# A streaming prefix log-sum-exp on one core: unrolled schedule against a hardware loop of four turns

## The chip, the core and the metric

The kernel runs on one core of a Trainium2 chip. The core has a matrix engine (PE), a vector engine (DVE), an activation engine (ACT), a general engine (POOL) and a sync engine (SP), which here does nothing but issue DMA transfers. Sixteen DMA engines move data between the device memory (DRAM) and the on-chip memory. The metric is the device time of one execution in microseconds.

## The reference

Input `x` and output have the shape [4, 4096, 4128] in fp32: four batches, 4096 time steps, 4128 independent columns. Along the time steps each column keeps a running log-sum-exp:

```python
out[:, 0, :] = x[:, 0, :]
for t in range(1, S):
    mx = np.maximum(out[:, t - 1, :], x[:, t, :])
    out[:, t, :] = mx + np.log(np.exp(out[:, t - 1, :] - mx) + np.exp(x[:, t, :] - mx))
```

That is the logarithm of the running sum of exp(x). Both kernels compute it in that form: Exp, prefix sum along the steps, Ln.

## The kernel before

A batch's 4096 steps are cut into tiles. A tile has r consecutive steps per partition, on 128 partitions, so 128 x r steps by all 4128 columns; r is `R` = 3 (6.34 MB) except for one tile of r = 2 per batch, since 4096 / 128 = 32 = 10 x 3 + 2. The tile of r = 2 is the first of batch 0 and the last of the other three (L150 to L153). That makes 11 tiles per batch, 44 in all. Each tile is loaded into one of four buffers, worked on in place, and stored from there.

The columns of a tile are cut into four chunks of 1024 (`CH`); the 32 columns left over, the tail, belong to the last chunk. The work on a chunk:

- `act` with Exp on ACT (L106), over all r steps; for the last chunk it covers the tail too;
- `own` on DVE (L77): r-1 adds that form the running sum inside each partition's r steps;
- `head` on PE (L74): two matrix products of 512 columns with the constant matrix `excl`, which sum each partition's last step over all partitions above it, into the chunk's own PSUM tile `above`;
- `add_above` on DVE (L77, one add of r x 1024 columns): adds that sum to every step;
- `pick` on PE (L74): two products with the constant `pick`, which copy partition 127's last step, now the running total, into `above` for the next tile, where `head` accumulates onto it;
- `act` with Ln on ACT, and after the last chunk's Ln the store.

The tail has no PSUM of its own: `above_t` is a piece of the last chunk's `above`. So its total is kept in SBUF in `carry_t` (L146), and for the last chunk `tail_head`, `tail_add` and half of `pick` stand in an order of their own: the tail's sum is written only after `add_above` has read that PSUM, and the last chunk's `pick` has to wait for `tail_add`.

The order of the work is written out by hand and fully unrolled (L183 to L199): for chunk g it issues `own` and `head` of chunk g+1, Exp of chunk g+2, `finish` (tail) and Ln of chunk g-1, and then `add_above` and `pick` of chunk g. This runs on without a break over tiles and batches: Exp of the next tile's first three chunks stands on ACT before the last chunk's Ln of this tile. A framework sets the semaphores.

SP's queue holds the three loads at the start, and then for each tile its store, followed by the load of the tile three further on (L173 to L177). That load goes to the buffer of the tile before the one just stored, so it waits until that store has landed. The constants `excl` and `pick` are made on POOL (L16 to L31), `carry_t` is cleared on DVE (L69).

Of the kernel before, what the change touches and what calls it, by code (L numbers as in the profile page):

```python
# [1 line left out]

# [4 lines left out]

FP32 = mybir.dt.float32
ACT = mybir.ActivationFunctionType
P = 128  # L10
R = 3
CH = 1024
MM = 512


def _constants(nc, pool):  # L16

    excl = pool.tile([P, P], FP32, name="excl")
    nc.gpsimd.memset(excl, 1.0)  # L19

    nc.gpsimd.affine_select(  # L21
        out=excl, in_=excl, pattern=[[1, P]], compare_op=mybir.AluOpType.is_ge,
        fill=0.0, base=-1, channel_multiplier=-1,
    )
    pick = pool.tile([P, P], FP32, name="pick")
    nc.gpsimd.memset(pick, 0.0)  # L26
    nc.gpsimd.affine_select(  # L27
        out=pick, in_=pick, pattern=[[0, P]], compare_op=mybir.AluOpType.not_equal,
        fill=1.0, base=-(P - 1), channel_multiplier=1,
    )  # L30
    return excl, pick  # L31


@with_exitstack
def kernel(
    ctx: ExitStack,
    tc: tile.TileContext,
    x: bass.AP,
    out: bass.AP,
):  # L40

    nc = tc.nc
    B, S, D = x.shape
    assert S % P == 0  # L50
    n_main = D // CH
    tail = D - n_main * CH
    t0 = n_main * CH
    last = n_main - 1

    nc.scalar.preload_act_table_set("natural_log_exp_and_others")  # L56
    consts = ctx.enter_context(tc.tile_pool(name="consts", bufs=1))
    excl, pick = _constants(nc, consts)

    bufs = 4  # L60
    xpool = ctx.enter_context(tc.tile_pool(name="xpool", bufs=bufs))
    cpool = ctx.enter_context(tc.tile_pool(name="cpool", bufs=1))
    psum = ctx.enter_context(tc.tile_pool(name="psum", bufs=1, space=bass.MemoryType.PSUM))

    above = [psum.tile([P, CH], FP32, name=f"above{c}") for c in range(n_main)]

    above_t = above[last][:, CH - MM:CH - MM + tail]
    carry_t = cpool.tile([P, tail], FP32, name="carry_t")
    nc.vector.memset(carry_t, 0.0)  # L69

    ctx.enter_context(tc.manual_schedule())

    def mm(pt, w, rhs, start=False, stop=False):
        nc.tensor.matmul(pt, lhsT=w, rhs=rhs, start=start, stop=stop, skip_group_check=True)  # L74

    def add(o, a, b):
        nc.vector.tensor_tensor(out=o, in0=a, in1=b, op=mybir.AluOpType.add)  # L77

    class Step:


        def __init__(self, b, row, r):
            self.b, self.row, self.r = b, row, r
            self.first = row == 0
            self.final = row + P * r == S

        def dram(self, t):
            rows = t[self.b, self.row:self.row + P * self.r, :]
            return rows.rearrange("(p j) d -> p j d", j=self.r)

        def load(self):
            full = xpool.tile([P, R, D], FP32, name="xt")
            self.xt = full[:, :self.r, :]
            nc.sync.dma_start(out=self.xt, in_=self.dram(x))  # L94

        def store(self):
            nc.sync.dma_start(out=self.dram(out), in_=self.xt)  # L97

    class Chunk:
        def __init__(self, step, c):  # L100
            self.t, self.c = step, c
            self.a, self.b = c * CH, D if c == last else (c + 1) * CH

        def act(self, func):
            v = self.t.xt[:, :, self.a:self.b]
            nc.scalar.activation(v, v, func)  # L106

        def own(self):

            x = self.t.xt  # L110
            for j in range(1, self.t.r):
                v = x[:, j, self.a:self.b]
                add(v, x[:, j - 1, self.a:self.b], v)

        def head(self):

            t, a = self.t, self.a
            for s in range(0, CH, MM):
                mm(above[self.c][:, s:s + MM], excl, t.xt[:, t.r - 1, a + s:a + s + MM],
                   start=t.first, stop=True)  # L120

        def add_above(self):
            t, a = self.t, self.a
            v = t.xt[:, :, a:a + CH]
            add(v, v, above[self.c].unsqueeze(1).to_broadcast([P, t.r, CH]))

        def pick(self, s0=0, s1=CH):

            t, a = self.t, self.a
            if not t.final:  # L130
                for s in range(s0, s1, MM):
                    mm(above[self.c][:, s:s + MM], pick, t.xt[:, t.r - 1, a + s:a + s + MM],
                       start=True)

        def tail_head(self):
            t = self.t
            if not t.first:
                mm(above_t, pick, carry_t, start=True)
            mm(above_t, excl, t.xt[:, t.r - 1, t0:D], start=t.first, stop=True)

        def tail_add(self):
            t = self.t
            v = t.xt[:, :, t0:D]
            add(v, v, above_t.unsqueeze(1).to_broadcast([P, t.r, tail]))
            if not t.final:
                nc.vector.tensor_copy(carry_t[96:, :], t.xt[96:, t.r - 1, t0:D])  # L146

    steps = []
    for b in range(B):
        n = S // P  # L150
        parts = [R] * (n // R) + ([n % R] if n % R else [])
        if b == 0:
            parts.reverse()  # L153
        row = 0
        for r in parts:
            steps.append(Step(b, row, r))
            row += P * r
        assert row == S

    chunks = [Chunk(s, c) for s in steps for c in range(n_main)]  # L160
    ahead = bufs - 1
    for s in steps[:ahead]:
        s.load()
    stored = 0
    def finish(k):
        if k.c == last:
            k.tail_add()
            k.pick(CH - MM)

    def result(k):  # L170
        nonlocal stored
        k.act(ACT.Ln)
        if k.c == last:  # L173
            k.t.store()
            if stored + ahead < len(steps):
                steps[stored + ahead].load()
            stored += 1  # L177

    chunks[0].act(ACT.Exp)
    chunks[1].act(ACT.Exp)  # L180
    chunks[0].own()
    chunks[0].head()
    for g, k in enumerate(chunks):  # L183
        if g + 1 < len(chunks):
            chunks[g + 1].own()
            chunks[g + 1].head()
        if g + 2 < len(chunks):
            chunks[g + 2].act(ACT.Exp)
        if g:
            finish(chunks[g - 1])  # L190
            result(chunks[g - 1])
        k.add_above()
        if k.c == last:
            k.tail_head()
            k.pick(0, CH - MM)
        else:
            k.pick()
    finish(chunks[-1])
    result(chunks[-1])  # L199


# [1 line left out]
_INS = ['x']  # L203
_OUTS = [((4, 4096, 4128), 'float32')]


# [23 lines left out]
```

The softmax here doesn't subtract the row's maximum and nothing guards it: scores larger than these inputs give would overflow.

## Time and profile before

| what | value |
|---|---|
| median of 10 runs | 1265.37 us (1263.63 to 1266.3) |
| profiled execution | 1265.5 us, its span 1263.8 us |
| moved by DMA | 541.35 MB, 428 GB/s over the span |
| DVE / ACT / PE busy | 980.2 / 923.9 / 755.9 us |
| load, store of r = 3: issue to landing | 41.2 us, 27.0 us (median) |
| load, store of r = 2: issue to landing | 36.2 us, 20.3 us (median) |

The span is the part that the profiler records; 1.7 us of the execution's time lie outside it. Busy time is that of an engine's own instructions. A tile of 6192 KB is listed as issued in one DMA, and the time to landing contains the wait behind earlier transfers in the same queue. GB/s counts reads and writes together.

### The profile page before, as it was taken

The page shows a single profiled execution, that of the slowest core. Times are in us where ns is not written, and L with a number is a line of the kernel's source. Part 1 is how long each engine was busy: PE and PEld are TensorE (multiplying, and loading weights), DVE is VectorE, ACT ScalarE, POOL GpSimd, SP SyncE. Part 2 cuts the span into 40 slices and gives each one's busy share as a digit, 9 for nine tenths or more (in the row PEclk, how much of TensorE's full clock was granted, in tenths as well). Part 3 has the DMA queues.
Part 4 walks back from the last instruction along what each step waited for, and adds up shares of the span by engine and source line. Part 5 has one row for each costly group of instructions (what it writes and reads, how often), then busy time and mean ns, then how long its engine had stood idle before and what let it go on. Part 6 is the DMA issues. An engine that isn't in the chain of part 4 may idle for free.

```text
span 1263.8 us, 4623 instructions
## 1 busy us (share of the span) xinstructions
PE 755.9 (60%) x1512; PEld 287.2 (23%) x1512; DVE 980.2 (78%) x597; ACT 923.9 (73%) x353; POOL 1.1 (0%) x8
## 2 busy tenths in 40 slices
PE   4676656554666666666366666666645666656562
PEld 1222222221222222222122222222212222222220
DVE  3998877777887878788579888787857978877793
ACT  4987666777777777767668777666866877666794
POOL 0000000000000000000000000000000000000000
PEclk9998888887788888888779888888878988888887
DMA  9999999999999999999999999999999999999998
GB/s 410 385 425 414 438 425 425 436 437 429 433 436 432 431 439 430 430 436 432 435 433 434 428 437 433 430 431 440 429 430 433 437 433 434 432 430 437 431 432 353
DMA packets 12694, 541.35 MB, mean 428 GB/s; under 512 B 1408, under 2 KB 1408, under 8 KB 1408
## 3 DMA queue, kind: packets, MB, share of 16 engines
q1 hardware_dynamic: 12672, 541.07, 99.4%
q8 instruction: 12, 0.20, 0.1%
q14 instruction: 10, 0.08, 0.0%
HBM read 270.53 MB, written 270.53 MB: 428 GB/s over the span
## 4 chain that ended last, share of the span: by engine, by line
DMA 67%; DVE 13%; PE 9%; ACT 8%; issue 1%; SPq 0%; ACTq 0%; DVEq 0%
DMA xt<-in_x_dram 63%; DVE xt L77 13%; PE above L74 9%; ACT xt L106 8%; DMA out_dram<-xt 4%; SPq L97 0%; DVE carry_t L146 0%; SPq L94 0%; ACTq L106 0%; DVEq L77 0%
## 5 line engine op out<-in xcount | busy, mean ns | idle before, releaser
L106 ACT ACTIVATE xt<-xt 128x3072 f32<-128x3072 f32 (+2 forms) x352 | 922.6, 2693 | 323.0 <-DMA xt<-in_x_dram 288.2
L74 PE MATMUL above<-xt,excl 128*128 128x512 f32 (+1 forms) x792 | 437.9, 680 | 348.1 <-DVE xt L77 338.7
L77 DVE TENSOR_TENSOR xt<-xt 128x1024 f32<-128x1024 f32 (+1 forms) x336 | 413.6, 1231 | 252.6 <-ACT xt L106 247.1
L77 DVE TENSOR_TENSOR xt<-xt,above 128x3072 f32<-128x3072 f32 (+3 forms) x220 | 582.9, 2651 | 10.5 <-PE above L74 9.0
L74 PE MATMUL above<-xt,pick 128*128 128x512 f32 x640 | 331.4, 631 | 131.2 <-DVE xt L77 131.2
L74 PEld LDWEIGHTS above<-xt,excl 128*128 128x128 f32 x792 | 161.0, 227 | 599.2 <-issue 487.4
L74 PEld LDWEIGHTS above<-xt,pick 128*128 128x128 f32 x640 | 113.9, 198 | 308.0 <-DVE xt L77 227.6
L74 PEld LDWEIGHTS above<-carry_t,pick 128*128 128x128 f32 x80 | 20.4, 265 | 50.8 <-DVE xt L77 48.0
L74 PE MATMUL above<-carry_t,pick 128*128 128x32 f32 x80 | 17.2, 304 | 10.2 <-DVE xt L77 10.2
L146 DVE COPY carry_t<-xt 32x32 f32<-32x32 f32 x40 | 7.1, 177 | 1.4
L56 ACT ACT_TABLE_LOAD x1 | 1.3, 1283 | 0.8 <-PEq L214 0.8
L69 DVE MEMSET carry_t<- 128x32 f32 x1 | 0.1, 85 | 0.9 <-PEq L214 0.9
L21 POOL TENSOR_SCALAR_AFFINE_SELECT excl<-excl 128x128 f32<-128x128 f32 x1 | 0.3, 292 | 0.0
L27 POOL TENSOR_SCALAR_AFFINE_SELECT pick<-pick 128x128 f32<-128x128 f32 x1 | 0.3, 292 | 0.0
L26 POOL MEMSET pick<- 128x128 f32 x1 | 0.2, 205 | 0.0
L19 POOL MEMSET excl<- 128x128 f32 x1 | 0.2, 204 | 0.3 <-POOLq L214 0.3
L214 POOL MEMSET const-bfloat16-1.0<- 128x1 bf16 x1 | 0.1, 102 | 0.0
L214 POOL MEMSET const-uint8-127<- 128x1 uint8 x1 | 0.1, 102 | 0.0
L214 POOL MEMSET const-float32-0.0<- 128x1 f32 x1 | 0.1, 99 | 0.3 <-issue 0.3
L214 POOL MEMSET const-float32-1.0<- 128x1 f32 x1 | 0.1, 99 | 0.0
## 6 DMA issues: line engine op xcount, KB each, us to landing
xt<-in_x_dram SPq DMA_DIRECT2D x40, 6192.0 KB, 41.2
out_dram<-xt SPq DMA_DIRECT2D x40, 6192.0 KB, 27.0
xt<-in_x_dram SPq DMA_DIRECT2D x4, 4128.0 KB, 36.2
out_dram<-xt SPq DMA_DIRECT2D x4, 4128.0 KB, 20.3
```

The costliest lines, as they stand in the source:

```text
L19: nc.gpsimd.memset(excl, 1.0)
L21: nc.gpsimd.affine_select(out=excl, in_=excl, pattern=[[1, P]], compare_op=mybir.AluOpType.is_ge, fill=0.0, base=-1, channel_multiplier=-1,)
L26: nc.gpsimd.memset(pick, 0.0)
L27: nc.gpsimd.affine_select(out=pick, in_=pick, pattern=[[0, P]], compare_op=mybir.AluOpType.not_equal, fill=1.0, base=-(P - 1), channel_mul ...
L56: nc.scalar.preload_act_table_set("natural_log_exp_and_others")
L69: nc.vector.memset(carry_t, 0.0)
L74: nc.tensor.matmul(pt, lhsT=w, rhs=rhs, start=start, stop=stop, skip_group_check=True)
L77: nc.vector.tensor_tensor(out=o, in0=a, in1=b, op=mybir.AluOpType.add)
L106: nc.scalar.activation(v, v, func)
L146: nc.vector.tensor_copy(carry_t[96:, :], t.xt[96:, t.r - 1, t0:D])
L214: nc = _bacc.Bacc("TRN2", target_bir_lowering=False, num_devices=1)
```

## The change

The schedule of one batch is written down once as three programs, one per compute engine, and each engine runs its program as a hardware loop of four turns, one turn per batch. Inside, every dependence between engines is a semaphore set by hand; at the end of a turn the counters are taken back to zero, and ACT waits for and takes back the four `loaded` counters. SP is not in a loop: its 48 loads and 48 stores are issued in the same order of store and load as before, with its own waits on `stored`.

A batch has 12 tiles: r = 2, then nine of r = 3, then 2, then 1, so three tiles per buffer in each turn. The schedule of a batch is closed: its last chunk's Ln stands before the next batch's first Exp.

The chunks of a tile now come in the order 3, 0, 1, 2, so that the chunk with the tail is first. The tail's PSUM is a piece of chunk 2's `above`, the last in the new order, and chunk 2's running total is kept in SBUF in a new tile `carry` [128, 1024], of which DVE copies 32 partitions after each `add_above`; `pick` then reads `carry` at the start of chunk 2's next `head`. Ln of chunk 2 waits for that copy. `add_above` of a chunk now stands ahead of Ln of the chunk before it. SP, like the compute engines, enters its part after a barrier that waits for DVE and POOL, and there are barriers behind it.

```diff
-    n_main = D // CH
-    last = n_main - 1
+    NC = D // CH
+    bufs = 4
+    n = S // P
+    rows = [2] + [R] * 9 + [2, 1]
...
-    bufs = 4
-    xpool = ctx.enter_context(tc.tile_pool(name="xpool", bufs=bufs))
+    xpool = ctx.enter_context(tc.tile_pool(name="xpool", bufs=1))
...
-    above_t = above[last][:, CH - MM:CH - MM + tail]
+    slots = [xpool.tile([P, R, D], FP32, name=f"xt{i}") for i in range(bufs)]
+    order = [NC - 1] + list(range(NC - 1))
+    lastc = order[-1]
+    above_t = above[lastc][:, :tail]
+    carry = cpool.tile([P, CH], FP32, name="carry")
     carry_t = cpool.tile([P, tail], FP32, name="carry_t")
+    nc.vector.memset(carry, 0.0)
     nc.vector.memset(carry_t, 0.0)
...
+        def head(self):
+            m = []
+            if self.c == lastc and not self.first:
+                m += [(o, pick, carry[:, s:s + MM], True) for o, v, s in self.banks]
+            m += [(o, excl, v, self.first) for o, v, s in self.banks]
+            after = chunks[-NC].tadd if self is chunks[-2] else None
+            self.h = T.put(lambda: mms(*m), self.o, after, to=V)
...
+            self.add_ = V.put(lambda: add(v, v, p), self.h, to=T if not self.final else None if self.tailed else A)
+            self.done = [self.add_] if self.add_.to is A else []
+            if self.c == lastc and not self.final:
+                self.done = [V.put(
+                    lambda: nc.vector.tensor_copy(carry[96:, :], self.x[96:, self.r - 1, self.a:self.a + CH]),
+                    self.add_, to=A)]
...
+    chunks = [Chunk(k, c) for k in range(tiles) for c in order]
...
     for g, k in enumerate(chunks):
-        if g + 1 < len(chunks):
-            chunks[g + 1].own()
-            chunks[g + 1].head()
-        if g + 2 < len(chunks):
-            chunks[g + 2].act(ACT.Exp)
-        if g:
-            finish(chunks[g - 1])
-            result(chunks[g - 1])
-        k.add_above()
-        if k.c == last:
-            k.tail_head()
-            k.pick(0, CH - MM)
-        else:
-            k.pick()
+        if g + 1 < N:
+            q = chunks[g + 1]
+            q.own()
+            q.head()
+        if g + 2 < N:
+            chunks[g + 2].exp()
+        k.add_above()
+        if g + 1 < N and chunks[g + 1].tailed:
+            chunks[g + 1].tail_head(k)
+        if k.tailed:
+            k.tail_add()
+        k.pick()
+        if g:
+            chunks[g - 1].ln()
+    chunks[-1].ln()
...
+            with eng.Fori(0, B):
+                for i, e in enumerate(prog.entries):
+                    if getattr(e, "load", None) is not None:
+                        k = e.load
+                        eng.wait_ge(loaded[k % bufs], 16 * (k // bufs + 1))
...
+                    ins = e.emit()
+                    if e.to is not None:
+                        ins.then_inc(sems[prog, e.to], 1)
+                if prog is A:
+                    for s in loaded:
+                        eng.wait_ge(s, 16 * per_slot).then_inc(s, -16 * per_slot)
...
+                for g in range(bufs - 1):
+                    load(g)
+                for g in range(total_tiles):
+                    i, k = g % bufs, g % tiles
+                    eng.wait_ge(sems[A, "sp"], g + 1)
+                    eng.dma_start(
+                        out=dram(out, g // tiles, k), in_=slots[i][:, :rows[k], :]
+                    ).then_inc(stored[i], 16)
+                    nxt = g + bufs - 1
+                    if nxt < total_tiles:
+                        if nxt >= bufs:
+                            eng.wait_ge(stored[nxt % bufs], 16 * (nxt // bufs))
+                        load(nxt)
```

## The prediction

> **What bounds the kernel now.** I read the slices of the page first, because they say which resource never rests.
>
> ```profile
> DVE  3998877777887878788579888787857978877793
> DMA  9999999999999999999999999999999999999998
> q1 hardware_dynamic: 12672, 541.07, 99.4%
> ```
>
> The DMA engines are busy in every slice, while the page gives DVE 78%, ACT 73% and PE 60% of the span. The next view is the table of stretches (columns: PE, PEld, DVE, ACT and POOL busy, clock, DMA share, GB/s).
>
> ```profile
> 0.00:5.00 5.00, 0.00 (x0) 0.00 (x0) 0.09 (x1) 1.28 (x1) 1.09 (x8) 1.00 0.71 238
> 40.00:45.00 5.00, 3.67 (x9) 1.29 (x8) 4.97 (x4) 4.29 (x2) 0.00 (x0) 1.00 0.57 241
> 45.00:60.00 15.00, 10.27 (x25) 3.52 (x23) 14.90 (x9) 15.00 (x7) 0.00 (x0) 1.00 1.04 423
> 60.00:80.00 20.00, 14.64 (x29) 5.50 (x29) 18.94 (x13) 15.79 (x7) 0.00 (x0) 0.91 0.92 396
> 80.00:105.00 25.00, 16.91 (x36) 6.27 (x34) 20.09 (x12) 16.49 (x7) 0.00 (x0) 0.93 1.03 409
> 300.00:1200.00 900.00, 544.78 (x1078) 206.83 (x1078) 704.59 (x427) 659.42 (x251) 0.00 (x0) 0.87 1.00 433
> 1230.00:1240.00 10.00, 6.13 (x16) 2.56 (x16) 8.29 (x8) 10.00 (x5) 0.00 (x0) 1.00 0.69 297
> 1240.00:1264.00 24.00, 2.62 (x8) 1.20 (x8) 4.92 (x4) 6.40 (x4) 0.00 (x0) 0.61 0.88 378
> ```
>
> The plateau is 433 GB/s for 900 us. All 541.07 MB at that rate take 1249.6 us, so only about 14 us of the 1263.8 us span can be won at all. They lie at the ends: 40 to 45 us loses 5 x (433-241)/433 = 2.2 us, and 1230 to 1240 us loses 10 x (433-297)/433 = 3.1 us. In both places the queue ran dry because a store was issued late. The waits say why stores are late elsewhere without harm:
>
> ```profile
> SPq L97 <- ACT xt L106: 1194.0, 44, 31.0
> ACT xt L106 <- DMA xt<-in_x_dram: 288.2, 42, 12.0
> ```
>
> SP waits for the Ln that completes a tile, ACT waits for loads. The timelines of ACT and of SP around the end of the second batch give the cadence:
>
> ```profile
> 597.34 17.22 ACT L106 ACTIVATE xt<-xt 128x2048 f32<-128x2048 f32 x8 [2.08 <-DMA xt<-in_x_dram]
> 626.60 18.91 ACT L106 ACTIVATE xt<-xt 128x3072 f32<-128x3072 f32 x8 [12.04 <-DMA xt<-in_x_dram]
> 655.90 13.38 ACT L106 ACTIVATE xt<-xt 128x3072 f32<-128x3072 f32 x5 [10.39 <-DMA xt<-in_x_dram]
> 680.26 13.38 ACT L106 ACTIVATE xt<-xt 128x3072 f32<-128x3072 f32 x5 [2.14 <-DMA xt<-in_x_dram]
> ...
> 610.93 0.34 SPq L97 DMA_DIRECT2D out_dram<-xt  x1
> 672.76 0.34 SPq L97 DMA_DIRECT2D out_dram<-xt  x1
> ```
>
> Call a tile's rows per partition r. Between the landings at 626.60 and 655.90 a store and a load of r=3 moved, 29.30/6 = 4.88 us per row; between 655.90 and 680.26 a store of r=2 and a load of r=3, 24.36/5 = 4.87. After load g+1 lands, ACT runs six operations and store g goes out: 610.93-597.34 = 13.59 us with r=2 behind r=3, 672.76-655.90 = 16.86 us with r=3 behind r=3. Meanwhile the queue holds store g-1 and load g+2. The lead is that work, less the 13.6 or 16.9 us, less the fixed latency (issue to first byte, last byte to semaphore). The last gap bounds the latency from above: work 14.6 us (store r=3 alone), store out at 13.59 us after landing (1223.59 to 1237.18), 3.1 us lost, hence 4.1. The first gap bounds it from below: work 14.6, store 0 out at 42.70-27.79 = 14.91, 2.2 lost, hence 1.9. I take 3. In full cadence the lead is 29.3-16.9-3 = 9 us.
>
> **The change part by part.** The sum is made against the profiled execution, 1265.5 us (span 1263.8 plus 1.7 around it), which lies 0.13 above the median, 1265.37.
>
> *Entry.* The first load is issued at 0.80 us now. In the new order SP first waits for POOL's constants and DVE's two memsets. POOL ends at 1.71. DVE starts at 0.88 and clears 128x1024 instead of 128x32 (0.09 us now): below, nothing past POOL; above, the 1.22 us of an add over 1024 columns, so 2.2. Two waits and two branches follow. I take the first load at 2.1: **+1.3 us**, bounds +0.9 to +3. Every later transfer moves with it.
>
> *First store.* It is at 42.70 because ACT, done at 39.46 with its sixth operation (27.79+11.67), waits 1.25 us for the tail: DVE's own adds of the next chunk, the tail add, then PE's pick. In the new order the tail went with the first chunk and Ln waits for DVE's above-add and the copy into `carry`. DVE: 30.6 + 2.5 (own adds) + 2.3 (above-add) + 1.2 (copy, priced as an add of 1024 columns; the 32x32 copy's 0.18 is the floor) = 36.6, before 39.46. The gap shrinks: **-1.25 us** (0 to -2.2). DVE is full from 40 to 60 us, so I follow it to store 1 (68.41 now): two `carry` copies add 2.4, but Ln no longer waits for 2.5 us of own adds, the tail and PE; about 65. Load 3 held the queue until about then, so I book nothing.
>
> *Carry copies.* 44 x 1.2 = 53 us more on DVE. A tile of r=3 costs DVE 4 x 2.48 + 4 x 3.35 + 0.43 = 23.8 us, then 25, in a cycle of 29.3: hidden by DVE's 247 us of waiting for ACT. Without that cover it would be 53 us.
>
> *Order on PE.* The third chunk's pick moves into the next head, 4 passes more in front of the above-add (about 2 us, 1.96 per four passes); own adds finish a chunk ahead, so DVE covers it.
>
> *Four more tiles.* Eight more DMAs, same bytes. ACT gets 32 more operations at a fixed part of 0.19 us (2750 ns at 3072, 1898 at 2048 columns), 6 us in all, inside 323 us idle. DMA: 4.87 against 4.88 us per row shows no price per transfer: 0; the upper bound is SP's own time to issue one, 8 x 0.34 = 2.7 us. The Trainium skill, "DMA: Bandwidth & Descriptors", section "Anatomy of one DMA", speaks against it: a fixed part of about 2.0 us per DMA, fitted on another issue path. By it eight DMAs would make the sum 16 us longer; the two cadences above show that a full queue hides it.
>
> *Small tiles: the leads.* With r = ...3,3,2,1 | 2,3,3... two stores have little queue ahead. The last r=3 store of a batch goes out 13.6 us after the r=2 load lands, while the queue holds a store of r=3 and a load of r=1: 4 x 4.87 = 19.5, lead 19.5-13.6-3 = 2.9 us. The first store of batches 2 to 4 sees a store of r=1 and a load of r=3: 2.9 again. Tightest latency (4.1) leaves 1.8. Cost 0. SP also stands longer at the `stored` waits there, with the store of r=1 and a load still queued.
>
> *Loop turns.* The last Ln issues before any Exp of the next batch, so ACT drains. Counted from the landing of the last r=3 load, load r=1 lands at 43.8, the final above-add ends about 59, the last Ln about 60, and the next batch's first load lands at 68.2 (14 rows x 4.87). So 8 us are free for the waits on `loaded`, the counter resets and the branch; then the second tile lands only at 92.5, and tile 0 needs about 15 of those 24. Cover 17 us per turn; cost 0. The row on fetching code: 12 instruction packets took 0.1% of 16 engines' span, 20 us, so 1.7 us each. The skill, "Runtime: NRT & Kernel Launch", section "Instruction fetch mechanics", says a taken branch out of the two-page window must fetch before it goes on. Fully exposed, three such fetches would make the sum 5 us more; the 8 us cover them.
>
> *End.* Now store 42 leaves the queue dry for 3.1 us. In the new order stores of r=3, 2, 1 follow the last loads. From the same zero the r=3 store goes out at 38 (queue full to 43.8), r=2 at 53 (full to 58.4), r=1 at 60 (full to 68): every lead is over 2 us. **-3.1 us** (-2 to -3.7).
>
> *Exit.* Two more barriers; the two at the end now take 0.6 us together: **+0.4** (0 to +1.5).
>
> Sum: 1.3-1.25-3.1+0.4 = -2.65; 1265.5-2.65-0.13 = **1262.7 us**, 0.21% under the median. What a measurement here can tell from no change is 0.2%, 2.5 us, so this sits on the bound; the likeliest case alone spans 1260.5 to 1264.5.
>
> **The rivals.** *Late stores at small tiles (slower).* The six operations carry more waits now. Seven places have a lead of 2.9 us. If Ln comes more than 2.9 us later than the 13.59 measured, each further us costs 7. At 16.9 us after landing, the r=3 figure, it costs 7 x 0.4 = 3, the sum 1265.6; at 18 us 7 x 1.5 = 10, the sum **1273**. For it: seven thin leads. Against: ACT shows no gap between operations (17.22 us for eight of r=2 and r=3), and DVE is ready first. It ends slower than before from 0.4 us of loss per place on.
>
> *The early loss goes too (faster).* 45 to 105 us loses 0.3+1.7+1.4 = 3.4 us more at 423, 396 and 409 GB/s. If that came from store 1, it goes with the 3 us that store 1 gains: **1259.3**. Against: load 4 lands at 103.78, too late for a dry queue alone.
>
> *Ends cancel (same).* Entry +3 and exit +1.5 at their upper bounds, gains as booked: 1265.5+4.5-4.35-0.13 = **1265.5**.
>
> **How the numbers follow.** Likeliest case 0.46 (0.29 beyond the bound on the fast side, 0.17 within), early loss gone 0.18, ends cancel 0.10, late stores 0.26 (0.25 slower, 0.01 within). Faster 0.47, same 0.28, slower 0.25. The range leaves about a tenth on each side: low 1258, just under the early-loss case; high 1273, the 18 us case of late stores.
>
> **What would show it.** Plateau of 433 GB/s unchanged; first load at about 2.1 us; store 0 about 13.7 us after load 1; no slice under 400 GB/s at the three turns, with ACT's longest wait there for a load; the last 40 us without the 297 GB/s dip. Wrong would be: dips near each turn (leads or the turn), a lower plateau (transfers have a price), or a first load past 4 us.

## The result and the profile after

The change makes the kernel slower: 1269.82 us (median of 8 runs, 1268.34 to 1271.42) against 1264.46 us for the kernel before beside it; ratio 1.0043, 95% interval 1.0034 to 1.0052. The profiled execution of the changed kernel spans 1269.0 us, 5.2 more than before.

The page of the changed kernel, its DMA rows (share of the 40 slices, GB/s, the data queue):

```profile
DMA  9999999999999999999999999999999999999997
GB/s 383 410 422 439 434 425 431 440 421 434 429 433 423 431 440 425 442 433 422 417 441 416 442 426 434 439 425 439 430 402 437 410 437 434 429 443 426 433 439 342
q1 hardware_dynamic: 13824, 541.07, 99.4%
```

The queue is as busy as before and moves the same bytes, yet slices 30 and 32 fall to 402 and 410 GB/s. The table of stretches of the changed kernel (columns as in the prediction) finds the places:

```profile
0.00:5.00 5.00, 0.00 (x0) 0.00 (x0) 0.95 (x2) 1.28 (x1) 1.09 (x8) 1.00 0.39 106
40.00:45.00 5.00, 4.53 (x7) 1.57 (x8) 4.94 (x5) 5.00 (x3) 0.00 (x0) 0.66 0.62 264
60.00:80.00 20.00, 14.02 (x29) 5.48 (x30) 19.77 (x14) 18.08 (x8) 0.00 (x0) 0.91 1.00 412
80.00:105.00 25.00, 18.48 (x39) 6.98 (x38) 23.96 (x16) 18.47 (x8) 0.00 (x0) 0.93 1.00 432
...
300.00:400.00 100.00, 60.48 (x124) 23.40 (x122) 68.72 (x47) 69.40 (x33) 0.00 (x0) 0.83 1.00 426
400.00:500.00 100.00, 67.59 (x125) 25.89 (x126) 85.70 (x56) 74.19 (x28) 0.00 (x0) 0.83 1.00 434
600.00:700.00 100.00, 64.61 (x135) 26.94 (x134) 65.53 (x47) 68.11 (x35) 0.00 (x0) 0.81 1.01 426
900.00:1000.00 100.00, 63.44 (x140) 26.04 (x141) 65.08 (x47) 66.48 (x36) 0.00 (x0) 0.86 0.99 418
```

Three things are seen. Nothing but 106 GB/s in the first 5 us: the entry. More than before from 60 to 105 us (412 and 432 against 396 and 409): a gain. And 426, 426 and 418 GB/s in the three stretches that hold a turn of the loop, with a DMA share of 0.99 or more: by that share the engines were not idle there, and yet their transfers took longer.

The trace also has the 16 completion marks of each transfer, one per DMA engine, and a record of each packet. From the last of the 16 marks of one transfer to the last of the next is the time a transfer took. In the plateau a load takes 14.56, 9.70 and 4.83 us for r = 3, 2 and 1, a store 14.66, 9.76 and 4.93. What is above that is called excess here. At these figures all the rows of either kernel take 1246.6 us; the rest of the span is excess, plus the time from the last landing to the end (0.83 us before, 1.62 after). But for rounding it adds up:

```
us of excess in                            before   changed   difference
first load (from the span's start)           3.4      5.0       +1.6
load 1 to load 4                             7.9      3.9       -4.0   (store 0 alone: 2.7, 1.4)
behind load 4, to load 9                     1.5      2.0       +0.6
three turns (tiles 9-15, 21-27, 33-39)       0.6      7.4       +6.8
all between and behind them                  2.9      2.5       -0.4
last landing to the end of the span          0.8      1.6       +0.8
sum                                                             +5.2
```

So the early gain paid for the entry and more; the turns made the kernel slower. SP's timeline around the second turn of the changed kernel (start, duration, issue):

```profile
602.16 0.34 SPq L289 DMA_DIRECT2D out_dram<-xt  x1
603.22 0.33 SPq L280 DMA_DIRECT2D xt<-in_x_dram  x1
616.45 0.34 SPq L289 DMA_DIRECT2D out_dram<-xt  x1
...
671.31 0.34 SPq L289 DMA_DIRECT2D out_dram<-xt  x1
671.70 0.43 SPq L280 DMA_DIRECT2D xt<-in_x_dram  x1
```

and ACT's timeline there, which shows the landings:

```profile
608.05 12.19 ACT L103 ACTIVATE xt<-xt 128x1056 f32<-128x1056 f32 x10 [2.26 <-DMA xt<-in_x_dram]
622.74 1.06 ACT L103 ACTIVATE xt<-xt 128x1024 f32<-128x1024 f32 x1 [2.50 <-ACTq L252]
633.42 7.36 ACT L103 ACTIVATE xt<-xt 128x2112 f32<-128x2112 f32 x4 [9.63 <-DMA xt<-in_x_dram]
657.74 16.20 ACT L103 ACTIVATE xt<-xt 128x3168 f32<-128x3168 f32 x7 [10.79 <-DMA xt<-in_x_dram]
```

The stores at 602.16 and 671.31 go out 602.16-588.59 = 13.57 us (588.59 is the landing of load 22) and 671.31-657.74 = 13.57 us after the landing that starts them, as predicted to 0.02 us. The loads ahead of them land at 608.03 and 677.28, so their leads are 5.9 and 6.0 us. And it is the load behind each of these two stores (the ones issued at 603.22 and 671.70) that takes 1.0 and 1.1 us more than its rows. The drained turn itself is covered: ACT's wait for the next batch's first load is 9.63 us long.

### The profile page after: what moved, and what is told of

It reads as the page before. It is cut to its first block, busy times and chain, and to the rows that moved or that the text cites. A ratio compares the mean times of both kernels' runs of the same rounds, so it can differ in the third digit from the quotient of the medians.

```text
span 1269.0 us, 4645 instructions
## 1 busy us (share of the span) xinstructions
PE 835.5 (66%) x1656; PEld 332.3 (26%) x1656; DVE 997.2 (79%) x650; ACT 926.2 (73%) x385; POOL 1.1 (0%) x8
## 5 line engine op out<-in xcount | busy, mean ns | idle before, releaser
L103 ACT ACTIVATE xt<-xt 128x3072 f32<-128x3072 f32 (+4 forms) x384 | 924.9, 2484 | 326.6 <-DMA xt<-in_x_dram 281.9
L111 PE MATMUL above<-xt,excl 128*128 128x512 f32 (+1 forms) x864 | 498.0, 707 | 330.5 <-DVE xt L106 329.7
L106 DVE TENSOR_TENSOR xt<-xt 128x1024 f32<-128x1024 f32 (+1 forms) x320 | 394.3, 1232 | 213.1 <-ACT xt L103 203.0
L111 PEld LDWEIGHTS above<-xt,excl 128*128 128x128 f32 x864 | 183.1, 231 | 557.4 <-DVE xt L106 396.3
L111 PE MATMUL above<-xt,pick 128*128 128x512 f32 x528 | 271.0, 637 | 51.9 <-DVE xt L106 51.3
L111 PEld LDWEIGHTS above<-xt,pick 128*128 128x128 f32 x528 | 103.9, 208 | 229.8 <-DVE xt L106 150.5
L111 PE MATMUL above<-carry,pick 128*128 128x512 f32 x176 | 86.9, 616 | 17.8 <-DVE xt L106 14.8
L111 PEld LDWEIGHTS above<-carry,pick 128*128 128x128 f32 x176 | 30.0, 189 | 74.1 <-DVE xt L106 45.9
L111 PEld LDWEIGHTS above<-carry_t,pick 128*128 128x128 f32 x88 | 19.5, 239 | 56.5 <-DVE xt L106 53.0
L162 DVE COPY carry<-xt 32x1024 f32<-32x1024 f32 x44 | 30.3, 690 | 1.5
L111 PE MATMUL above<-carry_t,pick 128*128 128x32 f32 x88 | 18.1, 292 | 15.3 <-DVE xt L106 15.3
```

What stands on the lines that cost most here:

```text
L103: return nc.scalar.activation(v, v, func)
L106: return nc.vector.tensor_tensor(out=o, in0=a, in1=b, op=mybir.AluOpType.add)
L111: m = nc.tensor.matmul(o, lhsT=w, rhs=rhs, start=start, stop=True, skip_group_check=True)
L162: lambda: nc.vector.tensor_copy(carry[96:, :], self.x[96:, self.r - 1, self.a:self.a + CH]),
```

## Experiments

In what follows the lead of a store is the time from its issue to the last mark of the load ahead of it in the queue, and the loss is the excess of the load behind it. Both go by the DMA engine that finishes last. Theory A is that a lead under some 7 us costs, because the engines that run ahead of the last then have nothing queued; B that the turn costs; C that each transfer costs.

**The loop undone.**

```diff
-            with eng.Fori(0, B):
+            for _turn in range(B):
+                seen = {}
```

> The changed kernel with its three programs written out four times instead of a hardware loop; same order, same waits and counter resets, same tiles. Theory A (thin leads: at each batch end two stores are issued so late that the DMA engines that run some 4 us ahead of the slowest have nothing queued, and the pair of transfers behind loses about 1 us each): nothing changes, 1269 to 1271 us, and the loads of tiles 12, 24 and 36 still land 0.4 to 1.2 us late. Theory B (the turn itself, that is branch, counter resets and code fetch, costs some 2 us): three turns come back, about 1263 us.

Measured: 1270.62 us, ratio to before 1.0043 (1.0027 to 1.0060), the same as with the loop. The six thin stores have leads of 5.9 to 6.0 us and their loads lose 0.75 to 1.45 us each. Its page shows the code being fetched all along, where the loop's does not. First the unrolled kernel, then the changed one, the rows on instruction packets (count, MB, share):

```profile
q8 instruction: 13, 0.21, 0.1%
q14 instruction: 10, 0.08, 0.0%
```

```profile
q8 instruction: 3, 0.05, 0.0%
q14 instruction: 3, 0.02, 0.0%
```

The loop saves those fetches and neither gains nor loses time by it. Theory B falls.

**Other places for the small tiles.**

```diff
-    rows = [2] + [R] * 9 + [2, 1]
+    rows = [2, 3, 3, 3, 3, 2, 3, 2, 3, 3, 3, 2]
```

> The changed kernel with the twelve tiles of a batch as 2,3,3,3,3,2,3,2,3,3,3,2 instead of 2, nine of 3, 2, 1. Still 48 loads and 48 stores, loop and turns as they are, but no store has less than five rows of other transfers ahead of it (7.5 us of lead before latency, as at the batch ends of the kernel before). Theory A (thin leads): the 6.8 us that the three turns lose go, about 1263 us. Theory B (the turn) and theory C (each extra transfer has a price): no change, 1269 to 1270 us.

Measured: 1265.18 us, ratio 1.0005 (0.9996 to 1.0015). The stretches that held 426, 426 and 418 GB/s, in this kernel:

```profile
300.00:400.00 100.00, 58.18 (x120) 23.28 (x121) 74.05 (x49) 69.90 (x31) 0.00 (x0) 0.85 1.00 433
600.00:700.00 100.00, 63.25 (x121) 25.34 (x121) 73.87 (x49) 70.20 (x32) 0.00 (x0) 0.78 1.01 435
900.00:1000.00 100.00, 57.93 (x122) 23.05 (x121) 72.71 (x48) 68.98 (x31) 0.00 (x0) 0.86 1.00 433
```

The plateau is back, with the same loop, turns, barriers and 48 loads. The shortest lead between the start and the last loads is 8.2 us. One load (that of tile 36) still lost 0.8 us behind a lead of 8.3; single losses of this size stand behind long leads too, as in the kernel before, where load 31 lost 1.2 us behind a lead of 12.5. It falls 2 us short of the expected 1263. Its span, 1263.3 us, is 5.7 under the changed kernel's; the excess is 15.3 instead of 20.8 us. Theory C falls as well: it has the eight more transfers, and no loss to the kernel before.

**The small tiles alone, in the unrolled kernel before.**

```diff
-        parts = [R] * (n // R) + ([n % R] if n % R else [])
-        if b == 0:
-            parts.reverse()
+        parts = [2] + [R] * 9 + [2, 1]
```

> The kernel before, unrolled and running on over the batches, with only the tiles of a batch changed to 2, nine of 3, 2, 1. No loop, no barrier at entry or exit, old chunk order. Theory A (thin leads): the same two thin places per batch end, so about 6 to 7 us slower than before, 1270 to 1272 us. Theory B (the turn): within 1 us of before, 1264 to 1266 us. Theory C (a price per transfer): 8 more transfers, 1265 plus 8 times the price; with 0.8 us each 1271 us, so this run alone does not part A from C, the run with spread tiles does.

Measured: 1277.79 us, ratio 1.0096 (1.0076 to 1.0117): the direction of theory A, twice its size. Here the old chunk order makes the next store late too: stores 13, 25 and 37, the second of each batch, have leads of 2.8, 2.9 and 1.9 us, and the loads behind them lose 1.8, 2.0 and 1.2 us. The expectation had counted two thin places per batch end and there are three. The loss does not follow the lead pair by pair: the stores just ahead of these, 12, 24 and 36, have leads of 4.4 to 4.6 us and the loads behind them lose only 0.1 to 0.25; those at 9, 21 and 33 have 5.6 to 5.9 and lose 0.9 to 1.25. At 12, 24 and 36 it is the first of the 16 marks that comes late, 1.5 to 1.7 us in the store itself, while the last mark is on time. The new chunk order gives these three 8.5, 8.7 and 8.4 us of lead in the changed kernel.

**The dip at the end taken away.**

```diff
+        if b == B - 1:
+            parts = [R] * 10 + [1, 1]
```

> The kernel before with the last batch's tiles as ten of 3, then 1, 1 instead of 2, so that the queue is not empty behind the last loads and the dip to 297 GB/s at 1230 to 1240 us goes. The prediction's term (the dip costs 3.1 us): about 1261.4 us. The rival read from the landings (the DMA engine that is last never waited there, only those ahead of it did): no change, 1264 to 1265 us.

Measured: 1265.74 us, ratio 1.0008 (0.9999 to 1.0018); no gain. The stretch of 297 GB/s reads, in this kernel,

```profile
1230.00:1240.00 10.00, 10.00 (x25) 4.37 (x24) 4.26 (x6) 6.80 (x7) 0.00 (x0) 1.00 0.90 380
```

and nothing came of it. The marks of the last transfers of the kernel before say why (first and last of the 16 engines, us):

```
                    first      last
load 43 (r=2)      1218.16   1223.51
store 41 (r=3)     1232.80   1238.37
store 42 (r=3)     1253.05   1253.21
store 43 (r=2)     1262.79   1262.96
```

By then the engines are 5.6 us apart. Store 42 was issued at 1237.18: the first engine had finished store 41 at 1232.80 and was idle, the last one was still at work on store 41 and went from it straight into store 42 (1253.21-1238.37 = 14.84 us, a full transfer). The span ends with the last engine, and that one never waited.

**Stores held back in the plateau.** A chain on POOL between the last Ln and the store, at 28 stores far from small tiles, with three clears and with seven:

```diff
         if k.c == last:
+            if 5 <= stored and all(s.r == R for s in steps[stored - 1:stored + 3]) and stored + ahead < len(steps):
+                v = k.t.xt[:, 0, k.a:k.a + 8]
+                nc.gpsimd.tensor_copy(held, v)
+                for _ in range(3):        # 7 in the second kernel
+                    nc.gpsimd.memset(junk, 0.0)
+                nc.gpsimd.tensor_copy(v, held)
             k.t.store()
```

> The kernel before, with 28 of its 44 stores, all in the middle of a run of tiles of r = 3, held back by three clears of a scratch tile on POOL (about 3.4 us with their two small copies) between the last Ln and the store. The lead of these stores (issue to the landing of the load ahead of them) falls from about 12.4 to about 9 us. Theory A with its threshold between 6.2 and 7.4 us: no loss, 1264 to 1266 us. Rival (any later store costs, in proportion): 28 times some part of 3.4 us, over 1275 us.

> The same with seven clears (about 7 us): the lead of the 28 stores falls to about 5.4 us. Theory A: below the threshold, so each pair of transfers loses 0.4 to 1.2 us, less where the loss itself gives the next store more lead: 1275 to 1295 us, with all engines losing and the DMA queue never empty. The prediction's rule (latency of 3 us, at most 4.1, so a lead of 5.4 is enough): no change, 1264 to 1266 us.

Measured: 1265.25 us with three, ratio 1.0005 (0.9996 to 1.0015); 1280.51 us with seven, ratio 1.0129 (1.0114 to 1.0144). SP's waits, first with three clears and then with seven (total us, times, longest):

```profile
SPq L100 <- POOL xt L182: 98.8, 28, 3.9
```

```profile
SPq L100 <- POOL xt L182: 211.6, 28, 7.9
```

So the stores are 3.5 us late at no cost, or 7.6 us late at 16 us. Putting this beside the other kernels (lead by the last engine; loss of the load behind):

```
kernel, stores                           lead us       loss us
kernel before, 4 at batch ends           7.4 to 7.5    0.0
three clears, 28 held stores             8.1 to 9.3    0.0 to 0.4
small tiles spread, from 270 us on       8.2 and more  0.0 to 0.3, one 0.8
changed kernel, 6 at batch ends          5.9 to 6.5    0.4 to 1.2
unrolled copy of it, the same 6          5.9 to 6.0    0.8 to 1.5
seven clears, 28 held stores             4.2 to 6.2    0.0 to 2.0, median 0.6
```

In these kernels the step lies between 6.5 and 7.4 us. It is no sharp law for each pair: the load of one row behind stores 8, 20 and 32 of the changed kernel lost 0.6, 0.0 and 0.35 us at leads of 8.4 to 8.5, and below the step a pair may pass unharmed and the next one pay. The prediction's rule, that 4.1 us are enough, is refuted for leads counted to the last engine, where compute, tiles and order are those of the kernel before. The clears write to the on-chip memory while transfers pass, and the kernel with three shows that three of them cost nothing; that the other four cost by themselves is not excluded by these two runs, but the changed kernel loses at the same leads without any.

The first of the 16 marks tells more. By then it comes some 3 to 6 us before the last, so the engine that is first has that much less lead. Call the time from a store's issue to the first mark of the load ahead of it the front lead, and look at how late the store's own first mark comes:

```
kernel, stores                           front lead us   first mark late by us
kernel before, 4 at batch ends           2.3 to 3.4      0.0
three clears, 28 held stores             3.0 to 5.4      0.0 to 0.1
changed kernel, 6 at batch ends          0.6 to 2.1      1.0 to 0.2
small tiles alone, stores 12, 24, 36     0.3 to 0.4      1.7 to 1.5
seven clears, 28 held stores             -0.6 to 2.3     2.3 to 0.1
```

The less front lead, the later the first mark: at the six stores of the changed kernel the two add up to 1.6 to 2.4 us. So the engines that run ahead did run dry there, and an engine needs about 2 us from issue (an estimate from these sums, 1.6 to 2.6 us in the last three rows), within or a little under the prediction's 1.9 to 4.1. That the last engine, which was never dry, then loses 0.4 to 1.2 us in the load behind does not follow from this. Behind store 30 of the kernel with the dip taken away and store 31 of the kernel with another start (below) the load lost nothing, though their front leads were 1.6 us and their first marks 0.5 and 0.4 us late. Behind store 9 of the unrolled copy it lost 1.0 us, though the first mark was on time.

**The new chunk order alone, in the kernel before.** The core of the edit:

```diff
-    chunks = [Chunk(s, c) for s in steps for c in range(n_main)]
+    chunks = [Chunk(s, c) for s in steps for c in order]        # 3, 0, 1, 2
...
+            if self.c == lastc and not t.final:
+                nc.vector.tensor_copy(carry[96:, :], t.xt[96:, t.r - 1, a:a + CH])
...
+        k.add_above()
+        if g + 1 < len(chunks) and chunks[g + 1].c == last:
+            chunks[g + 1].tail_head()
+        if k.c == last:
+            k.tail_add()
+        k.pick()
         if g:
             result(chunks[g - 1])
```

> The kernel before with the new chunk order and nothing else: chunks 3, 0, 1, 2, the tail with the first chunk, the copy into carry, add-above ahead of Ln; tiles, unrolled order over the batches and the framework's waits as before. If the 4 us that the changed kernel gains between 40 and 105 us come from that order: store 0 about 1.25 us and store 1 about 3 us earlier, load 4 lands 4 us earlier, 1260 to 1261.5 us. Rival (they come from the new tiles or the hand-set waits): 1264 to 1265 us.

Measured: 1262.34 us, ratio 0.9985 (0.9976 to 0.9995), faster than the kernel before. Store 1 goes out at 63.83 instead of 68.41 us with a lead of 5.4 instead of 1.1, load 4 lands at 100.5 instead of 103.7, 3.2 us earlier where 4 were expected.

**Another start in the kernel before.**

```diff
         if b == 0:
-            parts.reverse()
+            parts = [1, 2] + [R] * 9 + [2]
...
-    for s in steps[:ahead]:
+    for s in steps[:bufs]:
         s.load()
...
-            if stored + ahead < len(steps):
+            if 0 < stored < len(steps) - ahead:
```

> The kernel before with batch 0 cut as 1, 2, nine of 3, 2, and with all four buffers loaded at the start instead of three. By the lead theory the 7.7 us that transfers lose between 40 and 105 us are late stores 0 and 1: store 0 then goes out near 28 us with load 3 still to land near 47 (lead 19 us), store 1 near 47 us with 5 us of lead, so 1 to 2 us are lost instead of 7.7: 1258 to 1260 us. Rival (the early loss is a property of the start, engines in step, not of late stores): 1264 to 1265 us.

Measured: 1262.11 us, ratio 0.9984 (0.9974 to 0.9994). Up to 105 us the transfers behind the first load lose 1.7 us instead of 7.9. It is still 2 us short of the expected 1258 to 1260: loads 5, 6, 8 and 11 lose 0.54, 0.73, 0.60 and 0.80 us while the engines drift apart, where loads 5 to 11 of the kernel before lose 1.8 in all.

**Both of them.** The edits of the last two kernels together:

```diff
-            parts.reverse()
+            parts = [1, 2] + [R] * 9 + [2]
...
-    chunks = [Chunk(s, c) for s in steps for c in range(n_main)]
+    chunks = [Chunk(s, c) for s in steps for c in order]        # 3, 0, 1, 2
```

> Both edits of the last two runs in the kernel before: chunk order 3, 0, 1, 2 with the tail first, batch 0 cut as 1, 2, nine of 3, 2, four loads at the start. Lead theory: both act on the leads of stores 0 and 1, of which the second edit already cures most, so less than the sum of 1.8 and 2.0 us: 1260.5 to 1262 us. If the two gains have separate causes: the sum, about 1260 us.

Measured: 1262.08 us, ratio 0.9983 (0.9974 to 0.9992), no more than either alone: both cure the same stores. It is the lowest time of all, below the kernel before and the changed one, though no different from the two it is made of within the intervals.

**Ln ahead of Exp on ACT.** The line moved, first in the changed kernel, then in the kernel with both edits:

```diff
-        if g + 2 < N:
-            chunks[g + 2].exp()
         k.add_above()
...
         if g:
             chunks[g - 1].ln()
+        if g + 2 < N:
+            chunks[g + 2].exp()
```

> The changed kernel with one line moved: in ACT's program Ln of the chunk before now stands ahead of Exp of the chunk two on. After a load lands, the last Ln of the tile before then has two Exp and one Ln in front of it instead of three and two, so the stores at the batch ends go out some 9.3 instead of 13.6 us after the landing, and their leads rise from 6 to about 10 us, past the threshold. Tiles, loop, turns, barriers, number of transfers unchanged. Lead theory: the 6.8 us of the three turns go, and stores 0 and 1 come 4 us earlier too, which gives 1 to 3 us of the 3.6 that remain there: 1260 to 1263 us, below the kernel before in spite of 2.3 us of barriers. If the small tiles, the turn or the closed schedule cost by themselves: 1268 to 1270 us.

> The kernel of the first run of this set with that same line moved (Ln ahead of Exp). Lead theory: every lead is then above 10 us, so what is left beside the 1246.6 us of moving the rows is the first load's start (3.6 us), the end (0.8) and the drift of single engines (2 to 5 us): span 1253 to 1257, 1255 to 1259 us, the fastest of all. Rival: with the lead cured already, moving Ln gives nothing and its waits on PE can cost: 1260.5 to 1262 us as without it.

Both expectations were wrong: 1299.31 us, ratio 1.0268 (1.0242 to 1.0293), and 1266.72 us, ratio 1.0015 (1.0006 to 1.0024). In the first of the two the stores came later, not earlier. The wait of ACT in it, and in the changed kernel, where the line is not moved:

```profile
ACT xt L103 <- PE above L111: 289.4, 103, 6.4
```

```profile
ACT xt L103 <- PE above L111: 34.4, 21, 4.6
```

With Ln in front, ACT stands in its queue until PE and DVE are done with that chunk, and the Exp that would feed them stands behind it. The leads at the batch ends fell to 0.2, 0.0 and below zero, and elsewhere most lie between 3 and 12 us. So this kernel doesn't test whether a longer lead cures the changed one; the spread tiles do. It shows something else: behind a batch end its marks are only 1.1 us apart, and there stores 25 and 37 have leads of 4.0 us and their loads lose nothing, although six other stores near them, at 3.3 to 4.8 us, go with losses of 0.3 to 1.5. So the step at 6.5 to 7.4 us, measured with engines some 3 to 6 us apart, need not hold where they are closer.

In the second the leads did grow, from 8 to 16 us to 12 to 20 us from store 6 on, and nothing was gained by it: the transfers from store 3 to store 42 lose 5.1 us, against 5.3 without the moved line. What made it slower is the start, where store 2 goes out at 77.06 instead of 69.02 us and with the load behind it loses 5.5 us instead of 0.6, and the last two stores (2.1 instead of 1.1).

## Why the prediction was wrong

The prediction said 1262.7 us, 0.2% faster; it is 0.4% slower, inside the stated range and on the side of its slower rival. Its cadence held: 4.87 us per row, no price for eight more transfers, ACT's 13.6 us, and leads at the small tiles of 5.9 us before latency (measured 5.9 to 6.5). Step by step:

- *Small tiles: the leads.* This is the step that failed. "Lead 19.5-13.6-3 = 2.9 us ... Cost 0" takes the 16 engines as one, with a fixed latency of 3 us, bounded by 1.9 and 4.1. The 5.9 us before latency came out as forecast (5.9 to 6.5), but the turns cost 6.8 us instead of 0. The front engines had only 0.6 to 2.1 us, less than the 3 us, and their first marks came 0.2 to 1.0 us late; the last engine lost 0.4 to 1.2 us in the load behind. The same leads cost 16 us in all in the kernel with seven clears, and with the small tiles spread, at 8.2 us and more, the cost is gone. The upper bound of 4.1 was read from a rate over all 16 engines at a place where they are 5.6 us apart. The place and the sign were those of the rival *Late stores at small tiles*; its mechanism, a later Ln, was not.
- *End.* "-3.1 us" was booked for a gap of the first engines only, the second largest error of the sum. The last engine sets the end and had no gap; removing the dip gave nothing. GB/s over 16 engines showed a loss that was off the path.
- *First store.* -1.25 us, measured on store 0: 2.70 to 1.41, -1.3. Right, with its cause (13.58 us after landing instead of 14.91).
- *Store 1* was expected near 65 us and came at 65.65, but "I book nothing" was wrong by 2.7 us: its lead rose from 1.1 to 5.2 us, with the loss of the load behind it down from 2.1 to 0.2. This is the rival *The early loss goes too*, in good part, and the chunk order alone in the kernel before shows it.
- *Entry.* +1.3, measured 2.41-0.80 = +1.6. *Exit.* +0.4, measured +0.8.
- *Carry copies*, *PE's order*: hidden, as said; a copy takes 690 ns instead of the assumed 1.2 us.
- *Loop turns.* Cost 0 was right. The Trainium skill, "Runtime: NRT & Kernel Launch", section "Instruction fetch mechanics", would have a taken branch wait where its target is not in the two pages at hand; no run here shows such a wait: three large packets of code were fetched in all, and the unrolled copy takes the same time.

With the measured sizes put in (entry, start, turns, exit) and the end at nothing the same sum would have been 1265.4+1.6-4.0+6.8+0.8 = 1270.6. That the prediction came within 7 us of the result is in part luck: the early gain that it left out, 2.7 us, covers much of the 3.1 us that it booked for the end.

What stays open is why the load behind a late store costs the last engine time, when that engine was never dry. In the trace's packet records the loss sits in the last packets of that load, on most or all engines: of load 27 of the changed kernel, packets that take 1.83 us elsewhere took 2.0 to 3.0 us between 695.6 and 702.5 us. The DMA share counts such a packet as busy, so a share of 0.99 does not tell whether it waited. The branch and the number of transfers are excluded by the unrolled copy and the spread tiles; what holds the packets up was not tried.

## What to carry to other kernels

In a kernel bound by one DMA queue, list for every store how long the queue still has work when it is issued, counted to the engine that runs dry first and not to the last, and compare the shortest with what the old kernel is known to bear without loss; a lead outside what the trace has shown is an unknown, and not a cost of zero. Small tiles beside large ones take that lead away: they are short work in the queue ahead of a store that still needs a large tile's compute. A dip of the total rate is worth time only if the engine that finishes last has it.

## What the runs showed of the hardware

- The 16 DMA engines drift apart: the marks of one transfer lie within 0.7 us at the start and are 3.0 to 5.6 us apart from 160 us on, until the queue's end, in both kernels, and a queue that runs dry brings them together again (store 42 above: 0.17 us).
- With engines that far apart, the load behind a store issued 4.2 to 6.5 us before the last engine's work ends loses up to 2.0 us, and the DMA share does not show it; from 7.4 us on most lose nothing, though single ones lose up to 1.7 us even at a lead of 13 us (load 31 of the kernel with both edits).
- A store's first mark comes late when the front engine's work ends less than about 2 us after the store's issue (an estimate, from sums of 1.6 to 2.6 us).
- The same work as a loop (0.05 MB of code fetched in the larger instruction queue) and unrolled (0.21 MB) takes the same time within the intervals.
